# Gated linear attention products on all 128 rows: zero-padded queries, keys split by chunk parity, two heads in one product

## The chip, the cores and the metric

The kernel runs on one core of a Trainium2 chip, in one launch. The metric is the device time in microseconds, the median of several runs of the same program; a profile of one execution shows what each engine did.

## The reference

Two transformer-like blocks run one after the other on an input of 512 tokens by 1024 features, in float32. The first is: feed-forward, a mixer with two branches (S5 and gated linear attention, GLA), a second feed-forward, a norm. The second block has other mixers and is not touched. The change is in the GLA branch of the first block, which has 4 heads with keys of 64 and values of 128 features, and works on 8 chunks of 64 tokens:

```
log_a = log_sigmoid(a_low @ w_a_up + b_a_up) / 16
bcum  = cumsum(log_a within the chunk);  b_last = bcum at the chunk's end
q_t, k_t = qc * exp(bcum), kc * exp(-bcum)
scores   = causal(q_t . k_t)                     # 64 x 64 in a chunk
o_intra  = scores @ v
d_state  = (kc * exp(b_last - bcum))^T @ v       # 64 x 128 of a chunk
state    = exp(b_last) * state + d_state         # over the chunks
o_inter  = q_t @ state before the chunk
o = rms_norm(o_intra + o_inter) * silu(r)
```

## The kernel before

Activations lie with features on the 128 partitions and the 512 tokens along the columns. Every large matrix product is a sum of three products of float32r parts: weights and activations are split in a high and a low part, and `mm3` multiplies high by high, high by low and low by high. Each is 128 rows by 128 outputs by 512 columns and writes to a PSUM tile of the tag `mm` (4 buffers). A weight tile of 1024 columns is loaded through SP, copied to its high part by ACT and subtracted to its low part by DVE (`wsplit`). Small products, those of S5 and GLA among them, are in plain float32 and write to PSUM tiles of the tag `aux` (4 buffers). Most SBUF tiles come from one pool of 75 buffers of 512 columns, the tag `gen`.

The order of the instructions is not that of the program text. A `Recorder` notes every instruction with an engine, a cost, a class and its operands, plans them on a model of five engines in order of time, and issues them in the order of the plan. On each engine it takes the first that is ready and has a buffer, by class and by recorded order. The classes are URGENT, MAIN and BACK; `s5_run`, `gla_gate` and `gla_run` are recorded under BACK. On PE, products of BACK go ahead of others, but never two in a row when another is there (`streak`), so that they alternate with the large products. The cost of a product goes by its columns and type alone (line 404):

```
c = max(0.105, n * 0.42185e-3) if a.dtype == F32R else max(0.21, n * 1.68e-3)
```

POOL fills tiles with zeros (`zero`, line 389) and issues the loads of the S5 matrices (`s5w`), of `a_up` and of `cmask`. The argument `after` binds the plan only; on the chip a filling waits for its buffer alone. Every engine works through its instructions in order.

`mixer1` (line 927) computes the S5 input, then the low-rank gate (`al`, 16 rows), k, q, v and r, then the gates of the merge (16 large products), and last the projections, of which `proj_gla` reads the GLA outputs `yg`. `gla_gate` (line 1097) multiplies `wu` (16 rows, from `a_up`) by `al` and makes the decays E1, E2, E3 and `dec`. In `gla_run` (line 1130) `qt`, `kt` and `ke` hold two heads each, on partitions 0 to 63 and 64 to 127 for queries and keys. `ke` is transposed, tokens on partitions, two chunks in 128 rows. For each pair p of heads:

- line 1162 makes the state update of a chunk: the 64 rows of `ke` and `v` that belong to it, 256 columns for the values of both heads;
- line 1165 adds it to the decayed state, for each head in its 64 partitions;
- line 1171 makes the scores of one head, from the 64 rows of that head, 128 columns for two chunks;
- lines 1173 to 1176 keep the causal part in `sc`, by POOL's zeros and a copy under the mask by DVE;
- line 1181 multiplies values by `sc`, 128 rows; line 1185 adds state by query, 64 rows and 64 columns for each chunk and head.

Of the kernel before, what the change touches and what calls it, by code (L numbers as in the profile page):

```python
# [11 lines left out]
AF = mybir.ActivationFunctionType  # L12
# [25 lines left out]
# Columns of the packed per-feature vectors: name -> (first column, count).  # L38
# [17 lines left out]
# Constants that depend on shapes alone: name -> (first column, count).  # L56
# [17 lines left out]
class Recorder:  # L74
    """Records instructions, then issues them in the order of a list schedule: every engine takes the
    first instruction, by class and by recorded order, whose operands and buffers are there."""
# [19 lines left out]
    def op(self, eng, cost, emit, outs, ins, cls=None, table=None, nbytes=0, after=(), also=False):  # L96
        """also: writes another part of a tile that is being written already"""
        o = _Op()
        o.eng, o.cost, o.emit, o.table, o.nbytes = eng, cost, emit, table, nbytes
        o.seq = len(self.ops)  # L100
        c = self.cls if cls is None else cls
        o.back = eng == "pe" and c == BACK
        if o.back:
            c = URGENT
        o.key = (c, o.seq)
        o.users, o.left, o.ready, o.allocs = [], 0, 0.0, []
        deps = set()
        wn = [a.tensor.name for a in outs]
        rn = [a.tensor.name for a in ins]
        first = set()  # L110
        for n in rn + [a.tensor.name for a in after]:
            deps.update(self.writer.get(n, ()))
        for n in wn:
            if also:
                first.add(self.writer[n][0])
                continue
            if n in self.writer:
                deps.update(self.writer[n])
            elif n in self.tag:
                o.allocs.append(n)  # L120
            deps.update(self.readers.get(n, ()))
        for n in rn:
            self.readers.setdefault(n, []).append(o)
        for n in wn:
            if also:
                self.writer[n].append(o)
            else:
                self.writer[n] = [o]
                self.readers[n] = []
        o.tiles = {n for n in wn + rn if n in self.tag}  # L130
        for n in o.tiles:
            self.touch[n] = self.touch.get(n, 0) + 1
        deps.discard(o)
        first -= deps
        for d in deps:
            d.users.append((o, False))
        for d in first:
            d.users.append((o, True))
        o.left = len(deps) + len(first)
        self.ops.append(o)  # L140
        return o

    def schedule(self):
# [13 lines left out]
        order = []  # L157
# [4 lines left out]
        def blocked(o, t):  # L162
            """the tag that keeps o from starting at t, and when it may change"""
            for n in o.allocs:
                tag = self.tag[n]
                if tag in self.inorder and queue[tag][head[tag]] != o.seq:
                    return tag, None
                if not slots[tag]:
                    return tag, None
                if slots[tag][0] > t:  # L170
                    return tag, slots[tag][0]
            return None
# [120 lines left out]
def body(ctx, tc, A, out):  # L293
# [184 lines left out]
    def piece(w, n, k0, k1, after=()):  # L478
        """k-tiles k0 to k1 of w[n] in buffers of their own"""
        r = slot("pr")  # L480
        h = slot("ph", F32R)
        l = slot("pl", F32R)
        c = slice(0, (k1 - k0) * 128)
        dma("sp", r[:, c], A[w][n, :, k0 * 128:k1 * 128], after=after)
        act(h[:, c], r[:, c], AF.Copy)
        sub(l[:, c], r[:, c], h[:, c])
        return [(h[:, k * 128:k * 128 + 128], l[:, k * 128:k * 128 + 128]) for k in range(k1 - k0)]

    def linear(w, n, xs, after=()):
        """psum[128 n, 512] = sum over k of w[n, k]^T x[k]"""  # L490
        ps = mmps()
        kt = len(xs)
        nch = -(-kt // 8)
        edges = [kt * i // nch for i in range(nch + 1)]
        for k0, k1 in zip(edges[:-1], edges[1:]):
            h, l = wsplit(A[w][n, :, k0 * 128:k1 * 128], (k1 - k0) * 128, after=after)
            for k in range(k0, k1):
                c = slice((k - k0) * 128, (k - k0 + 1) * 128)
                mm3(ps, (h[:, c], l[:, c]), xs[k], k == 0, k == kt - 1)
        return ps  # L500

    def linear_pair(w, n, xs, after=()):
        """two neighbouring n-tiles with few k-tiles, one transfer"""
# [12 lines left out]
    def rsqrt(x, w):  # L516
        """x <- 1/sqrt(x), [128, w], by Newton steps from the bits"""
# [10 lines left out]
    def mean_sq(scale, eps, *ssum):  # L528
        """[128 tokens, T / 128] = scale * sum over features of all ssum + eps, ssum [128, T]"""
# [9 lines left out]
    def bcast(r):  # L539
        """psum with r[t] (compact [128, T / 128]) on every partition, [128, T]"""  # L540
# [15 lines left out]
    def norm_tile(h, g, i, st, hg):  # L556
        """what the next norm needs of feature tile i: gained parts and squares"""
# [16 lines left out]
    # ================= block 1 =================  # L574
    # the clock of the tensor engine rises with products that nobody reads, while the first loads run
# [70 lines left out]
    # final norm of block 1 and first norm of block 2 from the same tiles  # L646
# [25 lines left out]
    # ================= block 2 =================  # L672
# [11 lines left out]
    # the last tile and the final norm in two halves of the tokens  # L684
# [28 lines left out]
def s5_prep(env):  # L713
    """Discretized S5 parameters for chunks of four tokens, kept in DRAM until the mixer."""
# [47 lines left out]
    # angle, reduced to [-pi, pi] with a remainder  # L762
# [38 lines left out]
    # a - 1 = (|a| - 1) cos - 2 sin(theta/2)^2  # L801
# [21 lines left out]
    # table angles: 4 theta c with the leading bits of theta apart  # L823
# [8 lines left out]
    for b in range(4):  # L832
# [18 lines left out]
        # rotation tables  # L851
# [16 lines left out]
        # input and output matrices  # L868
# [34 lines left out]
        # causal products inside a chunk, with the skip term on the diagonal  # L903
# [23 lines left out]
def mixer1(env):  # L927
# [9 lines left out]
    # s5 input, written token-in-chunk major  # L937
# [16 lines left out]
    # gla low-rank gate, k, q, v  # L954
    G = {}
# [5 lines left out]
    al = slot("al")  # L961
    mul(al[0:16], ps[0:16], rB[0:16])
# [13 lines left out]
    # v, token major  # L976
# [31 lines left out]
    # s5 output gate  # L1008
# [12 lines left out]
    # merge  # L1021
# [13 lines left out]
def s5_run(e, U, res):  # L1035
    """S5 on chunks of four tokens; appends gelu(y) per feature tile, whole and split."""
# [60 lines left out]
def gla_gate(e, G):  # L1097
    """Decays from the low-rank gate: exp(b), exp(-b), exp(b_last - b), exp(b_last)."""
# [3 lines left out]
    e.dma("pool", wu[0:16, 0:256], e.A["a_up"], after=[e.rB])  # L1102
# [3 lines left out]
    for i in range(2):  # L1106
        ps = e.auxps()
        c = slice(i * 128, i * 128 + 128)
        e.mm(ps, wu[0:16, c], al[0:16], True, True)
# [20 lines left out]
def gla_run(e, G, yg):  # L1130
    nc, slot, act, mul, sub, stt = e.nc, e.slot, e.act, e.mul, e.sub, e.stt
    qt, kt, ke, v, dec = [], [], [], G["v"], G["dec"]
    for i in range(2):
# [6 lines left out]
        x = slot("ke")  # L1140
        act(x, pt, AF.Copy)
        ke.append(x)
        kt.append(k)
        mul(q, q, G["E1"][i])
        qt.append(q)

    for p in range(2):
        # states before each chunk of 64, two heads side by side
        Sx = [slot("S"), slot("S")]
        e.zero(Sx[0][:, 0:128], after=[ke[p]])  # L1150
# [4 lines left out]
        for c in range(7):  # L1155
            if c % 2 == 0:
                pd = e.auxps()
            t, rr = c // 2, slice((c % 2) * 64, (c % 2) * 64 + 64)
# [3 lines left out]
            e.mm(o, ke[p][rr, kc], v[t][rr, vc], True, True)  # L1162
# [3 lines left out]
        for hd in (2 * p, 2 * p + 1):  # L1166
            rr = slice((hd % 2) * 64, (hd % 2) * 64 + 64)
            pc = e.auxps()
            for t in range(4):
                c = slice(t * 128, t * 128 + 128)  # L1170
                e.mm(pc[:, c], kt[p][rr, c], qt[p][rr, c], True, True)
            sc = slot("sc")
            e.zero(sc, after=[pc])
            for t in range(4):
                c = slice(t * 128, t * 128 + 128)
                e.pick(sc[:, c], e.smask, pc[:, c])
            po = e.auxps()
            vc = slice(hd * 128, hd * 128 + 128)
            for t in range(4):
                c = slice(t * 128, t * 128 + 128)  # L1180
                e.mm(po[:, c], v[t][:, vc], sc[:, c], True, False)
                for q in range(2):
                    n = 2 * t + q
                    cq = slice(n * 64, n * 64 + 64)
                    e.mm(po[:, cq], Sc(n)[rr], qt[p][rr, cq], False, q == 1)
            o, sq = slot("o"), slot("osq")
            act(o, po, AF.Copy)
# [6 lines left out]
def lru_coef(e):  # L1194
    """-8 softplus(-lam) and its negative; softplus(x) = max(x, 0) + log1p(exp(-|x|)),
    log1p(y) = 2 atanh(y / (2 + y))"""
# [65 lines left out]
def pool_tile(e, n, u, res):  # L1262
    """u minus its centred window mean; u is padded by 16 zeros on both sides"""
# [115 lines left out]
def _wlay(w):  # L1379
    """[K, N] -> [N/128, 128, K] with k-tile j in columns 128 j to 128 j + 128"""  # L1380
# [88 lines left out]
```

## Time and profile before

| | |
|---|---|
| time, median of 3 runs | 1836.72 us (1835.18 to 1836.8) |
| span of the profiled execution | 1833.7 us |
| time outside the span, median less span | 3.0 us |
| PE busy | 1819.7 us, 99% of the span |
| DVE busy | 1116.6 us, 61% |
| ACT busy | 781.7 us, 43% |
| POOL busy | 46.0 us, 3% |

The profile gives the span of its execution from the first instruction to the last; the time of that execution with what lies around it isn't given apart, so the span is set beside the median. Matmuls are pipelined and their ends are modelled in the trace: two of them overlap in the records, and what a product takes of PE's time is read from the distance between starts. PEld is the loading of weights, which the trace shows apart. A float32 product appears as two records.

### The profile page before, as it was taken

The numbers are of one execution on the slowest core, as the hardware profiler recorded it, in microseconds if no ns is written. First come the engines' busy times: TensorE is split into PE (matmuls) and PEld (weight loads), VectorE is DVE, ScalarE is ACT, GpSimd is POOL, SyncE is SP. The second block draws the span as 40 slices with busy tenths as digits, with TensorE's granted clock in tenths as the row PEclk, the third lists the DMA queues.
The fourth block names the chain that finished last, engine by engine and source line by source line (L and its number), as shares of the span: only waits on it lengthen the run. The fifth ranks groups of instructions, "written<-read, shape, count | busy, mean of one in ns | idle before, by whom it ended". The sixth has DMA issues, their size and how long they took to land.

```text
span 1833.7 us, 21227 instructions
## 1 busy us (share of the span) xinstructions
PE 1819.7 (99%) x8232; PEld 1494.7 (82%) x8232; DVE 1116.6 (61%) x1867; ACT 781.7 (43%) x1016; POOL 46.0 (3%) x111
## 2 busy tenths in 40 slices
PE   9999999999999999999999999999999999999997
PEld 7888888888678888888888888888888888888886
DVE  7788853349554375444443349788765577777334
ACT  5344432223423333332323333899973344444222
POOL 0000000021000000000000001000000000000000
PEclk9999999999999999999999999999999999999999
DMA  4334433373212322222223323322223222222331
GB/s 173 119 138 138 135 117 95 103 260 121 69 35 92 103 93 97 96 95 97 99 89 97 101 93 131 105 83 85 81 80 115 92 97 98 92 104 89 97 125 46
DMA packets 66101, 191.47 MB, mean 104 GB/s; under 512 B 7553, under 2 KB 16401, under 8 KB 66001
## 3 DMA queue, kind: packets, MB, share of 16 engines
q1 hardware_dynamic: 60144, 171.49, 28.0%
q0 software_dynamic: 5712, 18.63, 2.9%
q8 instruction: 64, 1.05, 0.2%
q14 instruction: 37, 0.30, 0.0%
q10 hardware_dynamic: 144, 0.00, 0.0%
HBM read 178.56 MB, written 11.53 MB: 104 GB/s over the span
## 4 chain that ended last, share of the span: by engine, by line
PE 98%; DVE 1%; ACT 1%; DMA 0%; issue 0%; SPq 0%; DVEq 0%
PE mm L405 92%; PE aux L405 6%; PE aux L408 1%; DMA pr<-in_ffn_w_dram 0%; DVE o L354 0%; ACT sg L399 0%; DVE zt L354 0%; ACT a L399 0%; ACT L399 0%; DVE zr L370 0%; SPq L413 0%; DVE sg L366 0%; DVE zi L354 0%; DVE wl L354 0%; DVE sg L370 0%
## 5 line engine op out<-in xcount | busy, mean ns | idle before, releaser
L399 ACT ACTIVATE wh<-raw 128x1024 fp32r<-128x1024 f32 (+2 forms) x314 | 322.1, 1026 | 756.0 <-PE mm L405 477.8
L405 PE MATMUL mm<-hgh,wh 128*128 128x512 f32 x1528 | 602.1, 394 | 0.0
L405 PE MATMUL mm<-hgl,wh 128*128 128x512 f32 x1528 | 602.0, 394 | 0.0
L405 PE MATMUL mm<-hgh,wl 128*128 128x512 f32 x1528 | 601.8, 394 | 0.0
L354 DVE TENSOR_TENSOR wl<-raw,wh 128x1024 fp32r<-128x1024 f32 (+2 forms) x314 | 370.2, 1179 | 167.8 <-ACT wh L399 164.2
L405 PEld LDWEIGHTS mm<-hgl,wh 128*128 128x128 f32 x1528 | 286.2, 187 | 61.1 <-issue 2.5
L405 PEld LDWEIGHTS mm<-hgh,wh 128*128 128x128 f32 x1528 | 286.3, 187 | 60.1 <-issue 1.7
L405 PEld LDWEIGHTS mm<-hgh,wl 128*128 128x128 f32 x1528 | 286.3, 187 | 59.6 <-issue 1.0
L405 PE MATMUL mm<-gh,wh 128*128 128x512 f32 x506 | 196.9, 389 | 0.0
L405 PE MATMUL mm<-gl,wh 128*128 128x512 f32 x506 | 196.9, 389 | 0.0
L405 PE MATMUL mm<-gh,wl 128*128 128x512 f32 x506 | 196.9, 389 | 0.0
L405 PEld LDWEIGHTS mm<-gh,wl 128*128 128x128 f32 x506 | 95.0, 188 | 19.9
L405 PEld LDWEIGHTS mm<-gh,wh 128*128 128x128 f32 x506 | 95.0, 188 | 19.7
L405 PEld LDWEIGHTS mm<-gl,wh 128*128 128x128 f32 x506 | 95.0, 188 | 19.6
L354 DVE TENSOR_TENSOR ub<-mm,rB 128x512 f32<-128x512 f32 x44 | 30.4, 690 | 85.9 <-PE mm L405 85.9
L354 DVE TENSOR_TENSOR ua<-mm,rB 128x512 f32<-128x512 f32 x54 | 37.3, 690 | 68.9 <-PE mm L405 67.2
L399 ACT ACT_TABLE_LOAD x57 | 73.1, 1283 | 7.1 <-DMA yf<-dram 5.0
L366 DVE SCALAR_TENSOR_TENSOR y<-t,vec,y 128x511 f32<-128x511 f32 x88 | 65.8, 748 | 3.9 <-ACT y L399 2.3
L354 DVE TENSOR_TENSOR gate<-mm,rB 128x512 f32<-128x512 f32 x32 | 22.0, 689 | 54.0 <-PE mm L405 53.9
L354 DVE TENSOR_TENSOR t<-mm,rB 128x512 f32<-128x512 f32 x44 | 30.3, 688 | 40.2 <-PE mm L405 39.5
L354 DVE TENSOR_TENSOR h<-mm,h 128x512 f32<-128x512 f32 x23 | 15.9, 691 | 59.5 <-PE mm L405 59.5
L405 PE MATMUL mm<-mgh,wh 128*128 128x512 f32 x128 | 49.8, 389 | 0.0
(302 smaller groups left out, 2125.6 us busy)
## 6 DMA issues: line engine op xcount, KB each, us to landing
raw<-in_ffn_w_dram SPq DMA_DIRECT2D x100, 512.0 KB, 3.2
raw<-in_w_in_dram SPq DMA_DIRECT2D x62, 512.0 KB, 3.2
raw<-in_w_up_dram SPq DMA_DIRECT2D x44, 512.0 KB, 3.2
raw<-in_ffn_w_dram SPq DMA_DIRECT2D x32, 448.0 KB, 3.2
raw<-in_w_out_dram SPq DMA_DIRECT2D x16, 512.0 KB, 3.2
s5w<-dram POOLq DMA_DIRECT2D x28, 256.0 KB, 5.9
raw<-in_w_down_dram SPq DMA_DIRECT2D x14, 448.0 KB, 3.2
raw<-in_p_a_dram SPq DMA_DIRECT2D x16, 320.0 KB, 2.8
```

Of the source, the lines that this page charges most:

```text
L354: R.op("dve", dve1(o), lambda: nc.vector.tensor_tensor(out=o, in0=a, in1=b, op=op), [o], [a, b])
L366: R.op("dve", dve1(o) + 0.06 * len(_aps(s)), lambda: nc.vector.scalar_tensor_tensor(out=o, in0=a, scalar=s, in1=b, op0=op0, op1=op1), [o], ...
L399: R.op("act", c, lambda: nc.scalar.activation(o, i, f, **kw), [o], _aps(i, scale, bias), table=TABLES.get(f), cls=cls, after=after)
L405: R.op("pe", c, lambda: nc.tensor.matmul(ps, a, b, start=start, stop=stop), [ps], [a, b])
L408: R.op("pe", 0.12, lambda: nc.tensor.transpose(ps, a, ident), [ps], [a, ident])
```

## The change

The gate product gets 128 rows: `al` and the 256 columns of `wu` are filled with zeros first, by POOL, and their first 16 rows are written as before. Transposed keys are kept in two tiles for each pair of heads, one with the rows of even chunks and zeros in the others, one for odd chunks; the state update multiplies all 128 rows. Queries times E1 are written to two tiles `qz` for each pair, in which each chunk has 128 columns, 64 for each head, with zeros in the partitions of the other head. One product then gives the scores of both heads for two chunks (256 columns), and one gives state by query of both heads for a chunk (128 columns). Values by `sc` write the columns of their head in the interleaved PSUM tile, with a gap. Scores and outputs of both heads of a pair are computed together, in two PSUM tiles each. The comments of the file became blank lines, so that the line numbers stay the same up to the first added line.

```diff
@@ mixer1
     al = slot("al")
+    e.zero(al, after=[ps])
     mul(al[0:16], ps[0:16], rB[0:16])
@@ gla_gate
     wu = slot("wu")
-    e.dma("pool", wu[0:16, 0:256], e.A["a_up"], after=[e.rB])
+    e.zero(wu[:, 0:256], after=[e.rB])
+    e.dma("pool", wu[0:16, 0:256], e.A["a_up"])
...
-        e.mm(ps, wu[0:16, c], al[0:16], True, True)
+        e.mm(ps, wu[:, c], al, True, True)
@@ gla_run
-        x = slot("ke")
-        act(x, pt, AF.Copy)
-        ke.append(x)
+        kz = []
+        for c in range(2):
+            x, cr = slot("ke"), slice(64 * c, 64 * c + 64)
+            e.zero(x, after=[pt])
+            act(x[cr], pt[cr], AF.Copy)
+            kz.append(x)
+        ke.append(kz)
         kt.append(k)
-        mul(q, q, G["E1"][i])
-        qt.append(q)
+        qz = []
+        for c in range(2):
+            x, cs = slot("qz"), slice(256 * c, 256 * c + 256)
+            e.zero(x, after=[G["E1"][i]])
+            x4 = x.rearrange("p (n a c) -> p n a c", n=4, a=2)
+            for a in range(2):
+                ar = slice(64 * a, 64 * a + 64)
+                mul(x4[ar, :, a], q[ar, cs].rearrange("p (n c) -> p n c", n=4),
+                    G["E1"][i][ar, cs].rearrange("p (n c) -> p n c", n=4))
+            qz.append(x)
+        qt.append(qz)
...
-            e.mm(o, ke[p][rr, kc], v[t][rr, vc], True, True)
+            e.mm(o, ke[p][c % 2][:, kc], v[t][:, vc], True, True)
...
-        for hd in (2 * p, 2 * p + 1):
-            rr = slice((hd % 2) * 64, (hd % 2) * 64 + 64)
-            pc = e.auxps()
-            for t in range(4):
-                c = slice(t * 128, t * 128 + 128)
-                e.mm(pc[:, c], kt[p][rr, c], qt[p][rr, c], True, True)
-            sc = slot("sc")
-            e.zero(sc, after=[pc])
-            for t in range(4):
-                c = slice(t * 128, t * 128 + 128)
-                e.pick(sc[:, c], e.smask, pc[:, c])
-            po = e.auxps()
-            vc = slice(hd * 128, hd * 128 + 128)
-            for t in range(4):
-                c = slice(t * 128, t * 128 + 128)
-                e.mm(po[:, c], v[t][:, vc], sc[:, c], True, False)
-                for q in range(2):
-                    n = 2 * t + q
-                    cq = slice(n * 64, n * 64 + 64)
-                    e.mm(po[:, cq], Sc(n)[rr], qt[p][rr, cq], False, q == 1)
+        v4 = lambda x: x.rearrange("p (n a c) -> p n a c", n=4, a=2)
+        v3 = lambda x: x.rearrange("p (n c) -> p n c", c=64)
+        pc = [e.auxps(), e.auxps()]
+        for t in range(4):
+            o = slice((t % 2) * 256, (t % 2) * 256 + 256)
+            e.mm(pc[t // 2][:, o], kt[p][:, t * 128:t * 128 + 128], qt[p][t // 2][:, o], True, True)
+        sc = [slot("sc"), slot("sc")]
+        for a in range(2):
+            e.zero(sc[a], after=[pc[0]])
+            for t in range(4):
+                n = (t % 2) * 2
+                e.pick(v3(sc[a][:, t * 128:t * 128 + 128]), v3(e.smask), v4(pc[t // 2])[:, n:n + 2, a])
+        po = [e.auxps(), e.auxps()]
+        for t in range(4):
+            u, n = t // 2, (t % 2) * 2
+            for a in range(2):
+                hd = 2 * p + a
+                e.mm(v4(po[u])[:, n:n + 2, a], v[t][:, hd * 128:hd * 128 + 128], sc[a][:, t * 128:t * 128 + 128],
+                     n == 0 and a == 0, False)
+            for q in range(2):
+                cq = slice((n + q) * 128, (n + q) * 128 + 128)
+                e.mm(po[u][:, cq], Sc(2 * t + q), qt[p][u][:, cq], False, n + q == 3)
+        for a in range(2):
+            hd = 2 * p + a
             o, sq = slot("o"), slot("osq")
-            act(o, po, AF.Copy)
+            for u in range(2):
+                act(v3(o[:, u * 256:u * 256 + 256]), v4(po[u])[:, :, a], AF.Copy)
```

## Rows read from the trace of the kernel before

**Rows 1.** The page: span, busy time of each engine, chain that ended last.

```profile
span 1833.7 us, 21227 instructions
...
PE 1819.7 (99%) x8232; PEld 1494.7 (82%) x8232; DVE 1116.6 (61%) x1867; ACT 781.7 (43%) x1016; POOL 46.0 (3%) x111
...
PE 98%; DVE 1%; ACT 1%; DMA 0%; issue 0%; SPq 0%; DVEq 0%
```

**Rows 2.** Waits of PE, whole span: waiter, releaser, us, times, longest.

```profile
PE aux L408 <- DVE rs L366: 3.2, 1, 3.2
...
PE aux L405 <- DVE al L354: 0.2, 1, 0.2
```

**Rows 3.** Stretches: us, busy by engine (count), granted PE clock, DMA share, GB/s.

```profile
400.00:460.00 60.00, 59.82 (x328) 48.92 (x327) 55.91 (x102) 19.63 (x22) 6.10 (x16) 1.00 0.42 132
460.00:560.00 100.00, 100.00 (x443) 68.80 (x442) 51.62 (x132) 36.35 (x51) 0.00 (x0) 1.00 0.17 55
```

**Rows 4.** By tile, GLA products: count, ns (min/median/max), first and last start, form.

```profile
L405 PE MATMUL aux<-al,wu x4: 587/640/692, 413.5 to 440.8; 16*128 16x512 f32 x4
...
L405 PE MATMUL aux<-q,S x64: 272/296/321, 492.2 to 541.0; 64*128 64x64 f32 x64
...
L405 PE MATMUL aux<-q,k x32: 272/322/374, 469.8 to 486.9; 64*128 64x128 f32 x32
...
L405 PE MATMUL aux<-sc,v x32: 270/273/275, 491.6 to 539.6; 128*128 128x128 f32 x32
...
L405 PE MATMUL aux<-v,ke x28: 375/428/481, 481.7 to 526.1; 64*128 64x256 f32 x28
```

**Rows 5.** Timeline of PE, 128-row products: start us, us, instruction.

```profile
407.74 0.38 PE L405 MATMUL aux<-U,s5w 128*128 128x128 f32 x2
...
410.90 0.38 PE L405 MATMUL aux<-U,s5w 128*128 128x128 f32 x2
...
464.02 0.39 PE L405 MATMUL mm<-wh,hgh 128*128 128x512 f32 x1
...
465.84 0.39 PE L405 MATMUL mm<-wh,hgl 128*128 128x512 f32 x1
```

**Rows 6.** Timeline of PE, products with 16 and 64 rows.

```profile
439.95 0.40 PE L405 MATMUL mm<-hgh,wh 128*128 128x512 f32 x1
...
441.66 0.39 PE L405 MATMUL mm<-hgh,wl 128*128 128x512 f32 x1
...
470.68 0.49 PE L405 MATMUL aux<-q,k 64*128 64x128 f32 x2
...
475.75 0.49 PE L405 MATMUL aux<-q,k 64*128 64x128 f32 x2
...
481.65 0.70 PE L405 MATMUL aux<-v,ke 64*128 64x256 f32 x2
...
482.70 0.70 PE L405 MATMUL aux<-v,ke 64*128 64x256 f32 x2
...
495.29 0.43 PE L405 MATMUL aux<-q,S 64*128 64x64 f32 x2
...
496.08 0.43 PE L405 MATMUL aux<-q,S 64*128 64x64 f32 x2
```

**Rows 7.** By tile: DVE's multiply of 128x512 and of 128x256.

```profile
L354 DVE TENSOR_TENSOR q<-q,z x2: 682/682/683, 467.6 to 470.1; 128x512 f32<-128x512 f32 x2
...
L354 DVE TENSOR_TENSOR o<-h,aux x14: 410/412/420, 1817.7 to 1828.8; 128x256 f32<-128x256 f32 x14
```

**Rows 8.** Waits of POOL, 330 to 560 us.

```profile
POOL s5w L413 <- PE aux L405: 25.3, 2, 23.3
...
POOL S L390 <- DVE zt L354: 10.1, 1, 10.1
```

**Rows 9.** By tile: the GLA outputs' last part made, and their first reader.

```profile
L354 DVE TENSOR_TENSOR ygl<-o,ygh x4: 682/682/691, 516.3 to 553.7; 128x512 fp32r<-128x512 f32 x4
...
L405 PEld LDWEIGHTS mm<-ygh,wh x32: 187/188/188, 663.8 to 684.9; 128*128 128x128 f32 x32
```

More of the change, by code (lines that the diff above doesn't have):

```diff
@@ L1139, in gla_run @@
             e.tr(pt[:, t * 128:(t + 1) * 128], G["E3"][i][:, t * 128:(t + 1) * 128])
-        x = slot("ke")
-        act(x, pt, AF.Copy)
-        ke.append(x)
-        kt.append(k)
-        mul(q, q, G["E1"][i])
-        qt.append(q)
+        kz = []
[5 more added lines that the diff above has]
+        ke.append(kz)
+        kt.append(k)
+        qz = []
[9 more added lines that the diff above has]
+        qt.append(qz)
     for p in range(2):
         Sx = [slot("S"), slot("S")]
-        e.zero(Sx[0][:, 0:128], after=[ke[p]])
+        e.zero(Sx[0][:, 0:128], after=ke[p])
         def Sc(c):
@@ L1157, in gla_run @@
                 pd = e.auxps()
-            t, rr = c // 2, slice((c % 2) * 64, (c % 2) * 64 + 64)
+            t = c // 2
             o = pd[:, (c % 2) * 256:(c % 2) * 256 + 256]
```

## The prediction

> **What bounds the kernel now.** I read the page's busy line and chain first: PE is busy in 1819.7 us of a span of 1833.7 us and holds 98% of the chain that ended last [rows 1]. A busy PE need not be a PE at its peak, so the second view is the list of what PE waited for: five rows, together 7.0 us, the longest 3.2 us and the shortest, 0.2 us for the tile `al`, the only one in the GLA part [rows 2]. Hence time taken out of PE's stream comes out of the span, unless something new makes PE wait. The third view is the table of stretches: from 400 to 460 us DVE is busy in 55.91 of 60 us, so there PE has almost no lead to lose; from 460 to 560 us PE is busy throughout and DVE only half [rows 3]. The GLA products all lie between 413 and 541 us [rows 4]; after them the four outputs are complete at about 554 us, and their first reader runs at 663.8 us [rows 9]. So the latency of the GLA chain is worth nothing; only the PE time that its products take from the ordinary products between which they are placed counts.
>
> **What one product costs in PE's stream.** I take it from distances between starts, since the planner puts an ordinary product ("main", 128x512, three of which make one k-tile) after each background one. A float32 product shows as two records in the trace ("x2"). Main products alone: 8 distances from 464.02 to 465.84 us, 0.2275 us each. A main product and a float32 product with all 128 rows and 128 columns: 7 distances from 407.74 to 410.90 us, 0.451 us; the float32 product costs 0.224 us [rows 5]. The same with 64 rows: 6 distances from 470.68 to 475.75 us, 0.845 us; the product costs 0.617 us, 0.39 us more for half the rows. With 64 rows and 256 columns 481.65 to 482.70 us, 1.05 us, cost 0.823 us. With 64 rows and 64 columns 495.29 to 496.08 us, 0.79 us, cost 0.563 us. With 16 rows and 512 columns two main products and the gate product take 439.95 to 441.66 us, 1.71 us, cost 1.255 us [rows 6]. The full-row products stand in the same alternation, so it is not the alternation that costs the 0.39 us but the partial rows. The planner's cost of a product goes by columns alone (line 404), so its plan has never counted that 0.39 us.
>
> **The change part by part, on PE.** The trace has no full-row float32 product of 256 or 512 columns. Below: 0.224 us, if more columns cost nothing. Above: as many 128-column products, 0.448 and 0.896 us. I take the 128-column price plus what partial rows pay for more columns: 0.823 - 0.617 = 0.206 for 128 more, so 0.43 us; 1.255 - 0.823 = 0.43 for 256 more, so 0.86 us. Only the lower end is far, and the partial rows speak against it.
> - State times query: 64 records, so 32 products of 64x64, 32 x 0.563 = 18.0 us [rows 4, 6]. They become 16 of 128x128 (zeros in the padded queries keep the heads apart): 16 x 0.224 = 3.6 us. Gain 14.4 us.
> - Scores: 32 records, 16 products of 64x128, 16 x 0.617 = 9.9 us, become 8 of 128x256, 8 x 0.43 = 3.4 us. Gain 6.4 us (between 6.3 and 8.1).
> - State updates: 28 records, 14 products of 64x256; the number stays, rows become 128: 14 x (0.823 - 0.43) = 5.5 us (between 5.2 and 8.4).
> - Gate: 4 records, 2 products of 16x512, 2 x (1.255 - 0.86) = 0.8 us (between 0.7 and 2.1).
> - Values times scores: 32 records, 16 products that have 128 rows before and after. Their output is now two runs of 64 columns with a gap. No row shows such an output. Nearest are the 64-row products of 64 and 128 columns, 0.055 us apart: as two 64-column products each would cost 2 x (0.224 - 0.055) = 0.338 us, 0.114 us more, 1.8 us for all. That is the upper end, the lower is zero (a gap leaves no column out, so I exclude a gain). I take zero, because the count of columns, which the other rows follow, is unchanged.
>
> The sum is 14.4 + 6.4 + 5.5 + 0.8 = 27.1 us; with every lower column price it would be 32.8 us, with every upper price and the strided output 24.8 us.
>
> **What is added on the other engines.** DVE multiplies the queries in 8 pieces of 64x256 instead of 2 of 128x512: at 0.41 us (128x256) against 0.68 us that is 8 x 0.41 - 2 x 0.68 = 1.9 us more, in the backlog that ends near 470 us [rows 7]; the lower end is zero (equal element columns). The masking copies keep their number and size; their strided reading has no row, I take zero, and even doubled it lies after 470 us, where DVE is half idle [rows 3]. ACT copies the keys in 4 pieces instead of 2 and each output in two halves; this is some 3 us spread over stretches in which nothing on PE follows at once. POOL gets ten more fillings with zeros (`wu`, `al`, four `ke`, four `qz`), free in its time, but POOL works in order and issues the `s5w` loads: a load that waits for its buffer holds every filling behind it. Who waits for a filling is new: `al`'s filling precedes a DVE multiply, behind which DVE's whole queue stands, and the gate product, behind which all of PE's main products stand. The fillings of `qz` and `ke` can run before their data exist, as POOL has nothing else then. For `al` I charge 1 us on PE: the wait of 0.2 us shows that PE has no slack there [rows 2], and behind one load issue the filling comes late by that order. Its ends are zero (the filling runs ahead) and 23.3 us (it stands behind the longest wait on POOL's queue [rows 8]); I stay near zero, because `al`'s filling is recorded in the main class and the loads in the background one, so that the planner gives it POOL first. Buffers: the four `qz` and two more `ke` come when the S5 part gives its buffers back, and cost nothing unless that slips.
>
> So PE's stream loses 27.1 - 1.0 = 26.1 us. The profiled span of 1833.7 us becomes 1807.6 us. The median of the runs shown lies 3.0 us above that span, which I leave as it is: 1810.6 us, rounded 1811. Its own range is 1807 to 1815: a little of the cheaper columns on one side, the strided output (1.8 us), the DVE pieces (1.9 us) on the other.
>
> **A rule that speaks against it.** Main products of 128 rows follow each other every 0.2275 us [rows 5] although a weight load takes 1494.7 us / 8232 = 0.182 us on average [rows 1], so full-row loads do run beside products. The Trainium skill, "TensorE: Matmul & The Clock Gate", Part 3 (What overlaps and what doesn't), says that a weight load overlaps a product in flight only when its row group differs, by which a full-row product would always pay for its load. By this rule the change would give back 14.6 us; the trace disagrees, the distance of 0.2275 us being too short for load and product in turn.
>
> **The rivals.**
> - *The full rows pay for their loads.* The 40 new full-row products have 80 loads of 0.182 us, 14.6 us. 1836.7 - 27.1 + 14.6 = 1824. For it: the new ones are a mixture of sizes not in the trace. Against it: [rows 5]. The same case covers that the change doesn't do what it says, the price of partial rows staying in part. Chance 0.03.
> - *PE catches up with its feeders.* With 27 us gone, PE meets a DVE or a POOL that isn't ready: one wait like the 10.1 us for which POOL's filling of S waited for a buffer [rows 8]. 1836.7 - 27.1 + 10.1 = 1820. For it: DVE is full until about 470 us [rows 3]. Against: the planner counts full-row prices already, and DVE and ACT have room after 470 us. Chance 0.13.
> - *Slower than before, by POOL's queue.* The filling of `al` behind a load that waits 23.3 us, then a `qz` or `ke` filling behind a wait of 10.1 us, both on the way of PE's queue: 33.4 us of wait, 1836.7 - 27.1 + 33.4 = 1843. It decides from 30.8 us of wait (27.1 and the 3.7 us that 0.2% are). Against: both would have to lie wholly on PE. Chance 0.03.
> - *More gain.* Columns beyond 128 nearly free: 1836.7 - 32.8 = 1804 at the end, about 1806. Chance 0.04.
>
> **How the numbers follow.** The forecast has 0.77. Range 1807 to 1818: it holds the forecast's own range and the nearer part of the second rival, and leaves out somewhat under 2 in 10. About 0.2% (3.7 us) is what a measurement can tell from no change here: faster by more has 0.77 + 0.13 + 0.03 + 0.04 less 0.02 for waits that use up the gain, 0.95; within it 0.02; slower 0.03.
>
> **What the profile after would show.** No group with 64 or 16 rows among the `aux` products; 32 records of 128x128 with S, 16 of 128x256 with k, 28 of 128x256 with `ke`, 4 of 128x512 with `al`. State product and main product together every 0.45 us, 256 columns with main every 0.66 us. PE's list of waits still below some 8 us, the first reader of the GLA outputs near 637 instead of 663.8 us. Wrong would be: a distance over 0.6 us for state products, PE waiting on POOL or DVE for `al`, or a gain in the GLA stretch that is lost again before 664 us.

## The result

The kernel after takes 1809.32 us (median of 4 runs, 1809.27 to 1809.74); the kernel before, on the same chip, 1835.95 us (1834.87 to 1836.8). The ratio is 0.9854, 95% interval 0.9841 to 0.9867: 26.6 us less. The span of the profiled execution went from 1833.7 to 1808.0 us, 25.7 us less. The forecast was 1811 us.

The page of the kernel after (busy line, granted clock of the 40 slices, chain that ended last), against [rows 1]:

```profile
span 1808.0 us, 21155 instructions
...
PE 1794.4 (99%) x8184; PEld 1488.3 (82%) x8184; DVE 1117.2 (62%) x1873; ACT 783.2 (43%) x1022; POOL 50.6 (3%) x121
...
PEclk9999999999999999999999999999999999999998
...
PE 97%; ACT 1%; DVE 1%; issue 0%; DMA 0%; SPq 0%; DVEq 0%; ACTq 0%
```

PE is still the whole chain and still busy for 99% of the span; what changed is what it is busy with. By tile, the products with `al`, state, scores and keys, and the first reader of the GLA outputs (count, shortest, median and longest ns, first and last start, form), against [rows 4, 9]:

```profile
L405 PE MATMUL aux<-al,wu x4: 590/592/667, 418.5 to 441.1; 128*128 128x512 f32 x4
...
L405 PE MATMUL aux<-qz,S x32: 270/272/275, 486.2 to 518.3; 128*128 128x128 f32 x32
...
L405 PE MATMUL aux<-qz,k x16: 377/378/379, 474.3 to 506.2; 128*128 128x256 f32 x16
...
L405 PE MATMUL aux<-v,ke x28: 377/378/483, 477.0 to 506.8; 128*128 128x256 f32 x28
...
L405 PEld LDWEIGHTS mm<-ygh,wh x32: 187/188/188, 638.5 to 659.6; 128*128 128x128 f32 x32
```

No form with 64 or 16 rows is left. The first reader of the outputs runs at 638.5 instead of 663.8 us, 25.3 us earlier, so practically all of the gain was made before that point and kept to the end.

The price of the new products is read from distances between starts, as before. The timeline of PE in the kernel after (start us, us, instruction):

```profile
486.16 0.38 PE L405 MATMUL aux<-qz,S 128*128 128x128 f32 x2
486.30 0.47 PE L405 MATMUL mm<-hgl,wh 128*128 128x512 f32 x1
486.61 0.38 PE L405 MATMUL aux<-qz,S 128*128 128x128 f32 x2
...
503.98 0.59 PE L405 MATMUL aux<-qz,k 128*128 128x256 f32 x2
...
505.96 0.59 PE L405 MATMUL aux<-qz,k 128*128 128x256 f32 x2
```

State product and main product: 486.16 to 486.61 us, 0.45 us. Scores with main product: 3 distances from 503.98 to 505.96 us, 0.66 us each; less the 0.2275 us of the main product that is 0.43 us for 256 columns with full rows.

### The profile page after: what moved, and what is told of

It is laid out like the page before. It is cut to its first block, busy times and chain, and to the rows that moved or that the text cites. A ratio compares the mean times of both kernels' runs of the same rounds, so it can differ in the third digit from the quotient of the medians.

```text
span 1808.0 us, 21155 instructions
## 1 busy us (share of the span) xinstructions
PE 1794.4 (99%) x8184; PEld 1488.3 (82%) x8184; DVE 1117.2 (62%) x1873; ACT 783.2 (43%) x1022; POOL 50.6 (3%) x121
## 4 chain that ended last, share of the span: by engine, by line
PE 97%; ACT 1%; DVE 1%; issue 0%; DMA 0%; SPq 0%; DVEq 0%; ACTq 0%
PE mm L405 91%; PE aux L405 5%; PE aux L408 0%; DMA pr<-in_ffn_w_dram 0%; ACT L399 0%; DVE o L354 0%; ACT wh L399 0%; ACT zw L399 0%; ACT ke L399 0%; ACT sg L399 0%; ACT a L399 0%; DVE zw L366 0%; ACT v L399 0%; SPq L413 0%; ACT z L399 0%
```

## Why partial rows were dear: the loads of the weights

The prediction took the 0.39 us from distances without saying what it is. The trace of weight loads (PEld) shows it. In the kernel before, around one score product of 64 rows [rows 6]:

```profile
470.68 0.29 PEld L405 LDWEIGHTS aux<-q,k 64*128 64x128 f32 x2 [0.25 <-issue]
471.09 0.19 PEld L405 LDWEIGHTS mm<-wl,hgh 128*128 128x128 f32 x1
471.52 0.29 PEld L405 LDWEIGHTS aux<-q,k 64*128 64x128 f32 x2 [0.24 <-issue]
```

In the kernel after, around the state products shown above:

```profile
486.38 0.42 PEld L405 LDWEIGHTS aux<-qz,S 128*128 128x128 f32 x2
486.72 0.19 PEld L405 LDWEIGHTS mm<-hgh,wl 128*128 128x128 f32 x1
```

With full rows the load for the product that starts at 486.61 us begins at 486.38 us, 0.23 us ahead, under the main product before it; the loads follow each other without a gap. With partial rows the load begins at 470.68 us, the same moment as its product in [rows 6], after 0.25 us in which nothing is loaded. The load of the next main product again begins only with that product (471.09 us). That holds throughout: at all 128 changes between partial and full rows in the kernel before, from 400 to 560 us, the load begins 0 to 3 ns ahead of its product, and where full rows follow full rows 0.22 us ahead in the median. So loads run ahead while the row mode stays (all 128 rows, or only part of them), and not across a change of it. The Trainium skill, "TensorEngine Tiling (Array Packing)", Key Properties, states that changing the tiling mode drains the TensorE. The trace agrees in that no load passes such a change; the page gives no price, and here an excursion into 64 rows and back costs 0.39 us.

This leaves three theories of the price to be told apart. **A**: the 0.39 us belongs to each unbroken run of partial-row products, one way in and one way out, however many products it has. **B**: it belongs to each partial-row product. **C**: the rows don't matter, only that there are fewer products (24 fewer). The first group of experiments takes the kernel after and undoes one part of the change.

## Experiments: one part of the change undone

**State updates on 64 rows.** The key tiles with their zeros are made as in the kernel after; only the product reads half of them.

```diff
-            e.mm(o, ke[p][c % 2][:, kc], v[t][:, vc], True, True)
+            rr = slice((c % 2) * 64, (c % 2) * 64 + 64)
+            e.mm(o, ke[p][c % 2][rr, kc], v[t][rr, vc], True, True)
```

> The kernel after, but the 14 state updates multiply the 64 rows of their chunk again; the zero-filled key tiles are made as before, so that every other engine has the same work. Theories A and B: 14 x 0.39 us = 5.4 us more, about 1814.7 us, each update in a run of its own. Rival C (number of products) : no change, 1809 us. If PE had room there that other engines fill, less than 5.4 us would show.

Measured: 1814.69 us (1813.42 to 1815.99), 5.4 us more than the kernel after. The same products on the same data, with the same work on the other engines, cost 14 x 0.38 us more by their rows alone. C, which has nothing here, falls.

**Scores on 64 rows**, one head at a time, each head in a PSUM tile of its own:

```diff
-            o = slice((t % 2) * 256, (t % 2) * 256 + 256)
-            e.mm(pc[t // 2][:, o], kt[p][:, t * 128:t * 128 + 128], qt[p][t // 2][:, o], True, True)
+            n = (t % 2) * 2
+            for a in range(2):
+                rr = slice(a * 64, a * 64 + 64)
+                e.mm(pc[a][:, t * 128:t * 128 + 128], kt[p][rr, t * 128:t * 128 + 128],
+                     v4(qt[p][t // 2])[rr, n:n + 2, a], True, True)
...
-                e.pick(v3(sc[a][:, t * 128:t * 128 + 128]), v3(e.smask), v4(pc[t // 2])[:, n:n + 2, a])
+                e.pick(v3(sc[a][:, t * 128:t * 128 + 128]), v3(e.smask), v3(pc[a][:, t * 128:t * 128 + 128]))
```

> The kernel after, but the scores are made from 64 rows for one head at a time again, 16 products of 64x128 instead of 8 of 128x256, each head in a PSUM tile of its own; the rest stays. Theory A with each product in a run of its own: 16 x 0.617 - 8 x 0.43 = 6.4 us more, about 1815.7 us. Rival C (number of products alone): 8 more products at some 0.2 us, 1.7 us more, 1811 us.

Measured: 1815.71 us (1814.74 to 1816.67), 6.4 us more.

**Gate on 16 rows.**

```diff
-        e.mm(ps, wu[:, c], al, True, True)
+        e.mm(ps, wu[0:16, c], al[0:16], True, True)
```

> The kernel after, but the two gate products use 16 rows again; the fillings with zeros stay. Theory A: 2 x 0.39 = 0.8 us more, 1810.1 us. If the filling of al on POOL held PE up, its removal is not tested by this, since it is kept here; then nothing but the 0.8 us should show.

Measured: 1810.0 us (1809.2 to 1811.08), 0.7 us more; the difference is smaller than the spread of the runs, so this run alone doesn't show the gate's part.

**State by query not merged.** Full rows, but one product for each head.

```diff
-                cq = slice((n + q) * 128, (n + q) * 128 + 128)
-                e.mm(po[u][:, cq], Sc(2 * t + q), qt[p][u][:, cq], False, n + q == 3)
+                for a in range(2):
+                    cq = slice((n + q) * 128 + a * 64, (n + q) * 128 + a * 64 + 64)
+                    e.mm(po[u][:, cq], Sc(2 * t + q), qt[p][u][:, cq], False, n + q == 3 and a == 1)
```

> The kernel after, but the state-by-query products are not merged: 32 products of 128 rows and 64 columns instead of 16 of 128 columns; rows stay full. Theory A (rows decide): 32 products at 0.17 us (0.224 less the 0.055 us for 64 columns fewer) are 5.4 us against 3.8 us now, 1.6 us more, up to 3.4 us more if 64 columns cost as much as 128; 1810.5 to 1813 us. Rival C (the number of products decides, rows do not): 32 x 0.56 us = 18 us, 14 us more, about 1823 us.

Measured: 1813.63 us (1811.89 to 1814.44), 4.3 us more: far from the 14 us of rival C, and beyond the upper end of what A had. Its timeline shows why:

```profile
490.61 0.33 PE L405 MATMUL aux<-qz,S 128*128 128x64 f32 x2
...
491.97 0.33 PE L405 MATMUL aux<-qz,S 128*128 128x64 f32 x2
```

Three distances with a main product, 1.36 us, 0.453 us each: with full rows a float32 product of 64 columns takes the same time as one of 128. The 0.055 us that 64 columns fewer save on partial rows [rows 6] doesn't exist here. So 16 products more cost 16 x 0.225 = 3.6 us, and that part of the change's gain comes from the merging, not from the rows; the other 0.7 us of the 4.3 is within what the runs differ by.

## Experiments: the same partial rows in fewer runs

**Scores in runs of four.** The kernel before, with all its partial rows; the planner lets the 16 score products follow each other in fours, everything else alternates as before. The unbroken runs of partial rows fall from 64 to 52 (`...` marks lines left out).

```diff
...
-                if turn and o.back:
+                if turn and o.back and not (o.grp and grouped and streak < 4):
...
```

(`o.grp` marks a score product, `grouped` that the last product was one.)

> The kernel before; only the 16 score products (64 rows) come in four unbroken runs of four, everything else alternates with ordinary products as before. The unbroken runs of partial rows fall from 64 to 52. Theory A: 12 x 0.39 = 4.7 us less, about 1830.5 us, if the granted clock stays at 1.00 in the GLA stretch. Theory B: 1835 us. If the clock falls there, the first score runs still show about 0.22 us for a product that follows another.

Measured: 1830.52 us (8 runs, 1830.35 to 1832.46); ratio to the kernel before 0.9974, interval 0.9964 to 0.9985, by which it is 4.8 us less (2.8 to 6.6), where A said 4.7 and B nothing. The granted clock stayed at 1.00 from 400 to 560 us. The timeline of PE (the added lines make the helper's line 410):

```profile
469.50 1.16 PE L410 MATMUL aux<-q,k 64*128 64x128 f32 x8
470.58 0.49 PE L410 MATMUL mm<-wh,hgh 128*128 128x512 f32 x1
471.01 1.16 PE L410 MATMUL aux<-q,k 64*128 64x128 f32 x8
```

Four products of 64 rows and one main product take 1.51 us, against 4 x 0.845 us with a main product after each [rows 6]. Less 0.2275 us and 4 x 0.224 us, 0.39 us is left, once for the four. B falls: a partial-row product inside a run, on the same 64 partitions as the one before it, costs what a full-row one costs.

**All background products in runs of up to four, three and two**, in the kernel before, and up to four in the kernel after. One number is changed (4, 3 or 2 for 1):

```diff
-            turn = e == "pe" and streak >= 1
+            turn = e == "pe" and streak >= 4
```

> The kernel before with one number of the planner changed: up to four background products may follow each other on PE before an ordinary product is put between. The 64 partial-row products stay as they are, but come in 33 unbroken runs instead of 64. Theory A (the 0.39 us is paid on going into and out of partial rows, because weight loads don't run ahead across that change): 31 runs fewer x 0.39 us = 12 us less, about 1824 us, and a partial-row product that follows another costs close to the 0.224 us of a full-row one. Theory B (each partial-row product costs 0.39 us more wherever it stands): 1834 to 1837 us, unchanged.

> The kernel before with up to three background products in a row; 35 unbroken runs of partial rows. Theory A at full clock: 29 x 0.39 = 11.3 us less, about 1824 us. Theory D (long runs of small products lower the granted clock, and that is what took the gain from runs of four): between 1824 and 1840 us, with the clock at 0.50 for part of the GLA stretch; then runs of two should lose less than runs of three. Theory B: 1834 to 1837 us at full clock.

> The kernel before with up to two background products in a row instead of one. The 64 partial-row products come in 44 unbroken runs instead of 64. Theory A (each change into and out of partial rows costs 0.39 us): 20 x 0.39 = 7.8 us less, about 1827.5 us, if the granted TensorE clock stays at 1.00 in the GLA stretch; if it falls there as it did with runs of four, the time is lost again and the trace shows 0.50 in the stretch, while a product that follows another partial-row one still costs about 0.22 us there at full clock. Theory B (each product pays by itself): 1834 to 1837 us at full clock.

> The kernel after with the same number of the planner changed (runs of up to four background products). It has no partial-row product left, so under A and B alike it has next to nothing to gain: 200 background products at 13 ns (0.224 us against 0.213 us of streaming) are at most 2 us; 1807 to 1811 us. If it gains as much as the kernel before does from the same change (some 12 us), the gain there comes from the order of the work and not from the partial rows, and A falls.

Measured: the kernel before with runs of four 1838.96 us (ratio 1.0018, interval 1.0008 to 1.0027), of three 1834.42 us (0.9993, 0.9984 to 1.0003), of two 1841.75 us (1.0038, 1.0025 to 1.0052); the kernel after with runs of four 1810.11 us. The numbers alone look like theory B. The stretches (us, busy by engine and count, granted clock, DMA share, GB/s), first of the kernel before with runs of four, then of the kernel after with runs of four, say otherwise:

```profile
480.00:490.00 10.00, 10.00 (x51) 6.80 (x52) 5.67 (x14) 1.63 (x2) 0.00 (x0) 1.00 0.14 52
490.00:500.00 10.00, 10.00 (x49) 7.21 (x49) 3.45 (x17) 2.45 (x4) 0.00 (x0) 0.85 0.00 0
500.00:510.00 10.00, 10.00 (x31) 6.42 (x30) 4.79 (x22) 0.00 (x0) 0.00 (x0) 0.50 0.01 2
...
520.00:530.00 10.00, 10.00 (x33) 8.11 (x33) 3.20 (x13) 2.84 (x5) 0.00 (x0) 0.50 0.15 53
530.00:540.00 10.00, 10.00 (x42) 8.42 (x43) 5.77 (x19) 1.74 (x3) 0.00 (x0) 0.77 0.00 0
```

```profile
480.00:500.00 20.00, 19.73 (x114) 16.49 (x113) 15.49 (x58) 5.99 (x11) 0.00 (x0) 1.00 0.10 30
500.00:520.00 20.00, 20.00 (x118) 17.38 (x117) 12.76 (x40) 7.95 (x14) 0.00 (x0) 1.00 0.22 77
```

With partial rows the granted clock went from 1.00 (2.4 GHz) to 0.50 (1.2 GHz) shortly before 500 us and came back before 540 us. In these stretches PE was busy in 10.00 of 10 us throughout. With runs of three and two the trace shows 0.50 in 500 to 510 and in 500 to 520 us, and a second fall in 520 to 540 and in 530 to 550 us. With runs of four the time at 0.50 is some 37.5 us (497 to 534.5 us). An estimate from that: at half speed these 37.5 us hold work for half of them, so up to 18.7 us are lost, and A's 12 us saved and the 4 us by which the median came out above the 1835 us of before are 16 us. So the slower clock is enough to have taken what the fewer changes saved; that it did is argued from this sum, not shown by a run at full clock. In the kernel after with the same order the clock stayed at 1.00.

**What PE did before the clock fell.** Three kernels, all the kernel after with runs of up to four: the unmerged state products (full rows, as above), the scores and state updates on 64 rows (both diffs above), and state by query alone on 64 rows, one head and chunk at a time, each head in a PSUM tile of its own, so that values by `sc` write without a gap again:

```diff
...
-            for q in range(2):
-                cq = slice((n + q) * 128, (n + q) * 128 + 128)
-                e.mm(po[u][:, cq], Sc(2 * t + q), qt[p][u][:, cq], False, n + q == 3)
+                for q in range(2):
+                    n = 2 * t + q
+                    e.mm(po[a][:, n * 64:n * 64 + 64], Sc(n)[rr], v4(qt[p][t // 2])[rr, n % 4, a], False, q == 1)
...
```

> The kernel after with runs of up to four background products and 32 state-by-query products of 64 columns, all rows full: as many small products in as dense an order as in the kernel before with runs of four. Theory E (partial rows bring the granted clock down there): the clock stays at 1.00 in the GLA stretch, about 1814 us. Theory F (many small products in dense order bring it down, whatever their rows): 0.50 in part of the stretch, 1820 us and more.

> The kernel after with runs of up to four background products, and scores and state updates on 64 rows again: 30 partial-row products in 17 unbroken runs; state by query stays on full rows. At full clock, by theory A, 17 x 0.39 = 6.6 us more than the kernel after with runs of four, about 1817 us. Theory E: the granted clock falls in part of the stretch and the time is above that, up to 1835 us; theory F: the clock as in the kernel after with runs of four, 1.00.

> The kernel after with runs of up to four background products; only state by query is on 64 rows and 64 columns again, one head and chunk at a time (32 products in 18 unbroken runs, each head in a PSUM tile of its own); scores, state updates and gate stay on full rows. At full clock, by theory A, 18 x 0.39 = 7.0 us more than the kernel after with runs of four, and up to 3.7 us for the smaller products: 1817 to 1821 us. Theory E (it is these half-filled, short products in dense order that bring the granted clock down): 0.50 in part of the GLA stretch and 1825 us or more. If the clock stays at 1.00, neither kind of partial row does it alone, and what lowers it stays open.

Measured: 1813.33, 1814.0 and 1826.02 us (1823.56 to 1827.08). In the first two the granted clock is 1.00 in every stretch from 400 to 560 us. In the third:

```profile
500.00:510.00 10.00, 9.92 (x52) 7.60 (x50) 8.09 (x19) 3.20 (x5) 0.00 (x0) 1.00 0.22 61
510.00:520.00 10.00, 10.00 (x32) 7.55 (x33) 0.68 (x1) 2.46 (x4) 0.00 (x0) 0.56 0.12 46
520.00:530.00 10.00, 10.00 (x41) 8.62 (x40) 4.01 (x26) 0.43 (x1) 0.00 (x0) 0.59 0.00 0
```

So theory F (many small products in dense order, whatever their rows) falls by the first. Theory E in its wide form (any partial rows) isn't borne out by the second, whose 30 partial-row products stand in 17 runs. Of the three only the kernel with 32 products of 64 rows and 64 columns had the lower clock. Its first 16, from 480.4 to 489.7 us, ran with the clock at 1.00; it fell near 511 us, when ten of the second 16 had begun, and was back at 528 us. In the kernel before with runs of four it fell near 497 us, after 16 of them and among state updates of 64 rows. The measured 1826.0 us is 5 to 9 us over what A alone gave at full clock. In the kernel before, where a main product follows each of them, the clock stayed at 1.00. What it is in these products that goes with the fall stays open: the second kernel also has wider products, the third ran on another chip than the first two, and products of 64 rows and 128 columns in greater number weren't tried.

**Two halves at once.** The second kernel came out 2.7 us below what A gave from the same order on full rows (1810.1 + 6.6 = 1816.7 us). Its trace has a reason for a part of that. Its scores, in the order recorded, alternate between partitions 0 to 63 and 64 to 127:

```profile
469.43 0.71 PE L405 MATMUL aux<-qz,k 64*128 64x128 f32 x8
470.08 0.50 PE L405 MATMUL mm<-wl,hgh 128*128 128x512 f32 x1
```

Four products lie within 0.65 us of the next main product, against 1.08 us in the kernel with scores in fours shown above, where all four are on the same 64 partitions. Record by record, two of opposite halves start 6 to 7 ns apart and the next two 0.11 to 0.21 us later: they run at the same time. 9 such pairs of records are in this trace, 5 of scores and 4 of state updates; at 0.11 and 0.21 us each that is an estimated 1.4 us, and the rest isn't accounted for. The kernel before has none, as each of its partial-row products stands alone.

## Right and wrong, step by step

**What bounds the kernel**: right. Time taken out of PE's stream came out of the span, and what PE newly waited for in the GLA part is two rows, together 0.5 us:

```profile
PE aux L405 <- ACT ke L399: 0.3, 1, 0.3
PE aux L405 <- issue: 0.2, 1, 0.2
```

**The prices.** State by query: foretold 14.4 us. Scores: foretold 6.4, undone 6.4. State updates: foretold 5.5, undone 5.4. Gate: foretold 0.8, undone 0.7. The undone parts are 12.5 us together; of the 26.6 us measured 14.1 us remain for state by query with all that was added on other engines, against 14.4. This largest part is a remainder: no run put it back on 64 rows at full clock. By the prices above, 16 x 0.225 = 3.6 us of it are the merging and the rest the rows. The price of 256 columns, for which the trace of before had no row, was 0.43 us, as worked out from the slope of the partial rows. That of 512 columns was mis-sized: two main products and a gate product take 440.31 to 441.71 us, 1.40 us, so it costs 0.945 us, not 0.86. Set against these full-row prices, partial rows had cost 0.39 us more with 128 and 256 columns, 0.34 with 64 columns and 64 rows, and 0.31 with 512 columns and 16 rows. The output in two runs of columns with a gap cost nothing: values by `sc` and a main product come 0.46 us apart (484.12 to 484.58 us), against 0.451 for a product of this size without a gap [rows 5]. With every lower column price the prediction's parts add up to 33.0 us, not 32.8; nothing hangs on it. The timeline of PE in the kernel after:

```profile
440.31 0.48 PE L405 MATMUL mm<-hgh,wl 128*128 128x512 f32 x1
440.62 1.02 PE L405 MATMUL aux<-al,wu 128*128 128x512 f32 x2
441.08 0.79 PE L405 MATMUL mm<-hgh,wh 128*128 128x512 f32 x1
441.71 0.40 PE L405 MATMUL mm<-hgl,wh 128*128 128x512 f32 x1
...
484.12 0.38 PE L405 MATMUL aux<-sc,v 128*128 128x128 f32 x2
484.26 0.48 PE L405 MATMUL mm<-hgh,wl 128*128 128x512 f32 x1
484.58 0.38 PE L405 MATMUL aux<-sc,v 128*128 128x128 f32 x2
```

**The other engines.** DVE's pieces of 64x256 took 0.42 us each, as estimated (0.41). The filling of `al` was charged with 1 us and cost nothing: POOL ran it far ahead of the multiply into it.

```profile
L390 POOL MEMSET al<- x1: 545/545/545, 373.7 to 373.7; 128x512 f32 x1
...
L354 DVE TENSOR_TENSOR al<-mm,rB x1: 673/673/673, 413.6 to 413.6; 16x512 f32<-16x512 f32 x1
```

The loads that wait longest on POOL (22.5 us, up to 406.59 us) stand behind it. What PE did wait for was another addition, taken there as harmless: ACT's copies of the keys in four pieces with a table load between them, 0.3 us. The sum of 27.1 us less the gate's 0.2 and these waits of 0.5 is 26.4 us; the span shows 25.7. The remaining 0.7 us was not found in a row and is within what runs differ by. That the span came out at 1808.0 us against the 1807.6 foretold is in part luck: the 1 us charged for `al`, which cost nothing, made up for most of what wasn't foreseen (0.2, 0.5 and 0.7 us).

**From span to median**: wrong by 1.3 us. The 3.0 us set one execution's span against the median of others. The runs of the kernel after, each with its own span, give 1.7 to 1.8 us (1809.74 and 1808.0, 1809.27 and 1807.5); with these the sum would have said 1809.3 to 1809.4 us instead of 1810.6.

**The reason for the 0.39 us** was half right: alternation with full rows was excluded as its cause, because full-row products in the same alternation don't pay. It is alternation, but between row modes: partial rows pay only when the mode changes. For this change both readings give the same sum, since every partial-row product stood alone (64 runs for 64 products); for another cure, fewer changes of mode, only the second one forecasts the 4.8 us. It isn't the whole of it either: products on opposite halves can share the time, which neither reading has.

**The rivals.** That full rows pay for their loads is refuted by the loads that start 0.23 us ahead. PE catching up with its feeders took 0.5 us. POOL's queue made PE wait nowhere in the GLA part. More gain, by columns beyond 128 nearly free, is refuted by 0.43 us for 256 and 0.945 us for 512 columns against 0.224 for 128. The rule of the Trainium skill quoted against the change ("TensorE: Matmul & The Clock Gate", Part 3, What overlaps and what doesn't) doesn't hold here for a load of all rows behind a product of all rows: such a load starts 0.23 us before its own product, under the product ahead of it.

## What to carry to other kernels

Read a small product's price from the distance between starts, not from its own duration: 64 rows of 128 took 0.39 us more because the loads before and after it could not run ahead. Pad the rows with zeros where zeros already separate the data, or gather partial-row products in unbroken runs. Both take the same price away; after the second, check the granted clock of the stretch. In such a run let products on partitions 0 to 63 and 64 to 127 alternate: in one trace here such pairs ran at the same time. No run tried this instead of the zeros. A planner whose cost of a product goes by its columns can't see either, so look for forms with fewer rows in the trace.

## What had not been expected of the hardware

- A full-row float32 product costs PE the same 0.225 us with 64 and with 128 columns (0.453 and 0.45 us with a main product), so merging two short ones saves one of them entirely.
- An engine that the trace calls busy in 10.00 of 10 us can be at half clock: 0.50 to 0.59 in the slowest stretches of 10 us of the kernels in which 32 products of 64 rows and 64 columns stood in dense order, and 1.00 from 400 to 560 us in all others.
- One number of the order on PE, with the same products, moved the kernel before from 1835 us to between 1834 and 1842 us, and the same number in the kernel after changed its time by 0.8 us.
- Two float32 products of 64 rows on opposite halves of the partitions ran at the same time, 6 to 7 ns apart in their starts.
